# The first half of the value projection in 512-column matmuls, all of it ahead of the first attention scores

## The chip, the core and the metric

The kernel runs on one core of a Trainium2 chip. The metric is the device time of one execution in microseconds (us), the median of several runs. The engines of the core are named as in the profile: PE is TensorE (matmuls; PEld are its weight loads), DVE is VectorE, ACT is ScalarE, POOL is GpSimd, SP is SyncE, which here only issues DMAs.

## What is computed

The reference is a decoder trunk of two layers on 512 tokens of width 1024, in float32. Layer 0 mixes tokens by pooling, layer 1 by stick-breaking attention with 16 heads of 64 channels. Each layer is followed by a squared-ReLU MLP of width 4096, and every part sits between two RMS norms. What bears on the change is the shared key and value projection and the attention:

```python
kv = jnp.matmul(rms_norm(x, kv_norm_g), w_kv).reshape(B, S, 2, N_HEADS, HEAD_DIM)   # after layer 0
k = kv[:, :, 0].transpose(0, 2, 1, 3)
v = kv[:, :, 1].transpose(0, 2, 1, 3)
...
q = jnp.matmul(h, w_q[j])                                       # h = rms_norm(x, mix_pre_g)
log1m = jnp.where(mask, -jax.nn.softplus(z), 0.0)               # z = q k / 8, mask: s < t
excl = lax.cumsum(log1m, axis=3, reverse=True) - log1m
a = jnp.where(mask, jnp.exp(jax.nn.log_sigmoid(z) + excl), 0.0)
o = a @ v                                                       # per head
m = jnp.matmul(o, w_o[j])
```

## The kernel before, in words

**Numbers in two parts.** Every matmul operand is held as two tiles of a reduced float32 format, a high part (a cast on ACT) and a low part (a subtraction on DVE). A product is three matmuls: high by high, high by low, low by high. `mm3` (L299 to L302) issues them with a 128 x 128 block of activations as the loaded weights and a slice of weight columns as the moving operand; `up_block` (L703) the other way around, with weights loaded and up to 512 tokens moving.

**Weights.** The weights of the attention are read, multiplied by the norm gains, split in two parts and written back to DRAM (`kept`) during the MLP of layer 0 (`split_apart`, L207). The attention then only reads the two parts back, two DMAs of 512 KB a block (L242, on SP's queue). There are four slots for such blocks on the chip: three of the tag `w` and one of the tag `wx` (`place`, L190). `want` (L187) makes the list of blocks in the order in which the steps need them, `fill` (L246) reads the next ones while fewer than four are waiting to be used, and `get` (L253) takes one. The two blocks for the first step of the output projection are not kept; they are read raw and split on ACT and DVE (L170, L172).

**The order of attention.** The stage is a list of steps, `ATT_ORDER` (L59). The eight pairs of heads go through these steps; digits name a pair or unit, and the digits behind it token tiles of 128:

- `N2`, `N3`: the last two token tiles of the MLP's result are transposed on PE and split (`need`, L431). Tiles 0 and 1 were transposed inside the MLP's last step.
- `Vu...`: `values` (L882) for unit `u` of four heads, that is 256 columns. For a token tile it does 8 times `mm3` with 256 columns, and evacuates the PSUM bank by one cast on ACT (L897) and one subtraction on DVE (L898). A unit's weights are two blocks of four contraction chunks each.
- `K0`: `start` (L904) does the first 256 tokens of the key projection of pair 0 (24 matmuls of 256 columns), ahead of `N3`.
- `Pp`: `queries_keys` (L931) projects the keys and then the queries of pair `p`, 24 matmuls of 512 columns each (`project`, L910; for pair 0 the keys' other 256 tokens), and evacuates them with four casts and two subtractions for the keys (L936 to L938), two and two for the queries (L946, L947).
- `Sp`: `weights` (L1065): for each of the two heads, eight score matmuls (L991, L992) into three banks, sigmoids on ACT (L1000, L1012), a scan on DVE (L1016) and a multiplication on DVE (L1022).
- `Tp`: `transposed` (L1076): ten 128 x 128 transposes a head on PE (L1035) into three banks, and casts and subtractions of them (L1041, L1045).
- `Ap`: `mix_pair` (L1093): eight products with the values a head (L1052), one bank; evacuation on ACT and DVE (L1059, L1063) and a split (L281, L282).
- `Ou...`: `out_proj` (L1104): the output projection of two pairs. `E1`: the end of the stage, written out by hand.

The order on PE is written out by hand up to and including `P0` (`manual_schedule`, L1256). From there to the end step a planner of the framework sets each engine's order at build time, from the order of the program and from modelled times; the order that came of it is seen in the trace. All PSUM tiles come from one pool of 8 banks (`ps`, L123).

Of the kernel before, what the change touches and what calls it, by code (L numbers as in the profile page):

```python
# [10 lines left out]
F32 = mybir.dt.float32  # L11
F32R = mybir.dt.float32r
ACT = mybir.ActivationFunctionType
ALU = mybir.AluOpType

P = 128
D = 1024
S = 512
T = S // P
KC = D // P  # L20
# [7 lines left out]
HD = 64  # L28
# [4 lines left out]
TS = [slice(t * P, (t + 1) * P) for t in range(T)]  # L33
NS = [slice(0, 512), slice(512, 1024)]
# [23 lines left out]

ATT_ORDER = [  # L59
    (w[0], int(w[1]), [int(c) for c in w[2:]])  # L60
    for w in """V001 N2 K0 N3 V02 P0 V03 S0 P1 T0 V101 S1 A0 P2 T1 V123 A1 S2 P3 T2 O00123 A2 S3 P4 V201 T3 A3
    S4 P5 T4 V223 S5 A4 P6 V301 T5 S6 A5 V323 P7 T6 E1""".split()
]

# [37 lines left out]
C_MIX_PRE0, C_KV, C_MIX_PRE1, C_MLP_PRE1 = range(4)  # L102
# [3 lines left out]
def trunk(ctx, tc, x, consts, grow, pw, wup, wdn, wq, wk, wv, wo, out):  # L106
    nc = tc.nc
# [11 lines left out]
    def name(s):  # L119
        uid[0] += 1  # L120
        return f"{s}{uid[0]}"

    def ps():  # L123
        return psum.tile([P, 512], F32, tag="ps", name=name("ps"))
# [50 lines left out]
    def gains(lo, n):  # L175


        def scaled(raw):
            for k in range(n):
                c = raw[:, k * D // n : (k + 1) * D // n]  # L180
                nc.scalar.mul(c, c, gc[:, lo + k : lo + k + 1])  # L181

        return scaled

    gate, queue, made, ahead, dn_pool, att_pool, dn_raw = [False], [], {}, 4, [None], [None], {}

    def want(key, src, scaled=None):  # L187
        queue.append((key, src, scaled))
# [48 lines left out]
    def make():  # L237
        k, src, scaled = queue.pop(0)
        if k in kept:
            made[k] = place(k)  # L240
            for n, t in enumerate(made[k]):
                latest["sp"] = nc.sync.dma_start(t.bitcast(F32), kept[k][n])  # L242
            return
        made[k] = weight(src, place(k), scaled, dn_raw.pop(k, None))

    def fill(n=1):  # L246
        if gate[0]:
            behind.update(latest)
        for _ in range(n):
            if queue and len(made) < ahead and (queue[0][0][0] != "dn" or dn_pool[0]):  # L250
                make()

    def get(key):  # L253
        while key not in made:
            make()
        return made.pop(key)

    for l in range(2):
        if l == 1:
            n = len(queue)  # L260
            for what, i, part in ATT_ORDER:
                if what == "V" and 0 in part:
                    for h in range(2):
                        want(("v", i, h), wv[i, h], gains(C_KV * KC + 4 * h, 4))
                elif what == "P":
                    want(("k", i), wk[i], gains(C_KV * KC, KC))
                    want(("q", i), wq[i], gains(C_MIX_PRE1 * KC, KC))
                elif what == "O" or what == "E":
                    for c in range(2 * i, 2 * i + 2 if what == "O" else PAIRS):
                        want(("o", c), wo[c])  # L270
            apart.extend(x for x in queue[n:] if x[0] not in [("o", c) for c in range(2)])

            queue[n - GRP : n + GRP] = queue[n : n + GRP] + queue[n - GRP : n]
        for j in range(NJ):
            want(("up", l, j), wup[l, j])
        for j in range(NJ - GRP, NJ):
            want(("dn", l, j), wdn[l, j])
# [21 lines left out]
    def mm3(dst, ah, al, bh, bl, start, stop):  # L299
        nc.tensor.matmul(dst, ah, bh, start=start, stop=False)  # L300
        nc.tensor.matmul(dst, ah, bl, start=False, stop=False)  # L301
        nc.tensor.matmul(dst, al, bh, start=False, stop=stop)  # L302

    xnh = keep.tile([P, KC, S], F32R, tag="xnh", name="xnh")
    xnl = keep.tile([P, KC, S], F32R, tag="xnl", name="xnl")
# [125 lines left out]
    def need(*tiles):  # L431
        for t in tiles:
            if t in pending:
                pending.pop(t).transpose()
# [59 lines left out]
    def y_tiles():  # L494
        return [work.tile([P, D], F32, tag=f"y{t}", name=name(f"y{t}")) for t in range(T)]
# [207 lines left out]
    def up_block(pu, w, cols, last=False):  # L703
        wh = w[0].rearrange("p (k c) -> p k c", k=KC)
        wl = w[1].rearrange("p (k c) -> p k c", k=KC)

        def low(k):
            nc.tensor.matmul(pu[:, cols], wl[:, k, :], xnh[:, k, cols], start=False, stop=k == KC - 1)  # L708

        for k in range(KC):  # L710
            nc.tensor.matmul(pu[:, cols], wh[:, k, :], xnh[:, k, cols], start=k == 0, stop=False)  # L711
            nc.tensor.matmul(pu[:, cols], wh[:, k, :], xnl[:, k, cols], start=False, stop=False)  # L712
            if not last:
                low(k)
        if last:
            for k in range(KC):
                low(k)
# [161 lines left out]
    with tc.tile_pool(name="att", bufs=1, reuse_waits="tile") as ap:  # L879
        att_pool[0] = ap  # L880

        def values(u, part):  # L882
            if u not in vs:
                w = [get(("v", u, h)) for h in range(2)]
                vs[u] = w, ap.tile([P, T, 4, 2, HD], F32R, tag="v", bufs=2, name=name("v"))
            w, v = vs[u]
            for s in part:
                need(s)
                pv = ps()
                for k in range(KC):  # L890
                    c = slice((k % 4) * 256, (k % 4) * 256 + 256)
                    mm3(
                        pv[:, :256], xnh[:, k, TS[s]], xnl[:, k, TS[s]],
                        w[k // 4][0][:, c], w[k // 4][1][:, c], k == 0, k == KC - 1,
                    )
                pv4 = pv[:, :256].rearrange("p (h d) -> p h d", h=4)
                nc.scalar.copy(v[:, s, :, 0, :], pv4)  # L897
                nc.vector.tensor_tensor(  # L898
                    out=v[:, s, :, 1, :], in0=pv4, in1=v[:, s, :, 0, :].bitcast(F32), op=ALU.subtract
                )  # L900

        started = {}

        def start(key):  # L904

            need(0, 1)
            started[key] = ps(), get(key)
            up_block(*started[key], slice(0, S // 2))

        def project(key):  # L910
            need(*range(T))
            if key in started:
                pq, w = started.pop(key)
                up_block(pq, w, slice(S // 2, S))
            else:
                pq = ps()
                up_block(pq, get(key), slice(0, S))
            return pq

        def qk_tile(tag):  # L920
# [38 lines left out]
        with tc.issue_after(latest["pool"].ins):  # L959
            nc.gpsimd.memset(begin, 0.0)  # L960
            for lo, n in SEG.values():
                c = min(n - P, 1)
                d = begin[:, lo + n - P - c : lo + n]
                nc.gpsimd.affine_select(
                    out=d, in_=d, pattern=[[-1, P + c]], base=c - 1, channel_multiplier=1,
# [99 lines left out]
        def weights(p):  # L1065
            hs = [Head(qk[p], p, a) for a in range(2)]
            for x in hs:
                for b in range(3):
                    x.scores(b)
                    x.against(b)  # L1070
                    x.for_(b)
                x.scan()
                x.weigh()
            return hs

        def transposed(hs):  # L1076
            for x in hs:
                for b in range(3):
                    x.turn(b)
                    x.high(b)  # L1080
                    x.low(b)
# [20 lines left out]
        vs, os, wos, y = {}, {}, {}, y_tiles()  # L1102
# [119 lines left out]
        def until(key):  # L1222
            while key not in made:
                make()

        qk, heads, gpost1 = {}, {}, None

        def step(what, i, part):
            nonlocal gpost1
            if what == "V":  # L1230
                values(i, part)
            elif what == "N":
                need(i)
            elif what == "K":
                start(("k", i))
            elif what == "P":
                qk[i] = queries_keys(i)
                if i == PAIRS - 1:
                    until(("o", 5))
            elif what == "S":  # L1240
                gate[0] = True
                heads[i] = weights(i)
                fill()
            elif what == "T":
                transposed(heads[i])
                behind.update(latest)
            elif what == "A":
                mix_pair(i, vs[i // 2][1])
            elif what == "O" and part:
                out_proj(i, part)  # L1250
                if i == 0:
                    with tc.issue_after(latest["sp"].ins):
                        gpost1 = gain_row(R_MIX_POST1)

# [65 lines left out]
```

## Time and profile before

| | |
|---|---|
| Median of 3 runs | 952.17 us (951.81 to 952.43) |
| The profiled execution | 952.24 us, of which the span from first to last instruction is 950.5 us |
| Granted TensorE clock, mean over the span | 0.999 |
| First value step (V001) begins | 368.46 us into the span |
| First score of pair 0 (S0) begins | 392.91 us |
| Transposes of pair 2 (T2) begin | 454.31 us |
| First output projection (O0) begins | 456.41 us |

Times in the views are us from the start of the span. A timeline row gives the start, the time that the instruction took, the engine, the line of the kernel, the operation, what it writes and reads, the shapes and the count; in brackets stands the idle time of the engine before it and what ended it. Matmuls are pipelined, so a row's duration is longer than the distance to the next one's start; it is that distance that adds up. A windows row gives, for a stretch, the busy time of each engine and the number of its instructions.

### The profile page before, as it was taken

How to read it: one execution, taken by the hardware profiler on the slowest of the kernel's cores; microseconds unless marked ns; L12 is line 12 of the kernel's file. 1: busy time of each engine (PE TensorE's matmuls, PEld its weight loads, DVE VectorE, ACT ScalarE, POOL GpSimd, SP SyncE). 2: the span in 40 equal slices, each digit the busy share in tenths (PEclk: the TensorE clock that was granted, in tenths of full speed). 3: DMA queues.
4: the chain of work that ended last, by engine and by line, in shares of the span. 5: the costliest groups of instructions: out<-in, count | busy, mean ns of one | idle time of the engine just before them, and what ended most of it. 6: DMA issues, size and time to landing. Idle time of an engine off the chain costs nothing.

```text
span 950.5 us, 12510 instructions
## 1 busy us (share of the span) xinstructions
PE 940.9 (99%) x4758; PEld 799.7 (84%) x4758; DVE 707.9 (74%) x813; ACT 577.8 (61%) x1015; POOL 42.1 (4%) x85
## 2 busy tenths in 40 slices
PE   9999999999999999999999999999999999999996
PEld 7998888888888889899899988898888888888885
DVE  5875798988979976476577778874696966958756
ACT  6667979788775547456656554865545444444532
POOL 2300000000000004000000000200000000000002
PEclk9999999999999999999999999999999999999999
DMA  8244969789697760522424271442513233133102
GB/s 309 96 178 148 342 219 347 295 283 356 217 323 269 271 207 2 202 85 90 172 95 178 91 264 45 134 155 71 196 43 131 93 133 111 45 133 111 35 11 89
DMA packets 43262, 156.15 MB, mean 164 GB/s; under 512 B 4289, under 2 KB 4673, under 8 KB 43202
## 3 DMA queue, kind: packets, MB, share of 16 engines
q1 hardware_dynamic: 43202, 155.36, 46.1%
q8 instruction: 37, 0.61, 0.3%
q14 instruction: 23, 0.19, 0.1%
HBM read 121.79 MB, written 33.55 MB: 163 GB/s over the span
## 4 chain that ended last, share of the span: by engine, by line
PE 94%; DVE 2%; ACT 2%; POOL 1%; issue 1%; POOLq 0%; DVEq 0%; ACTq 0%
PE ps L589 28%; PE ps L708 15%; PE ps L712 15%; PE ps L711 15%; PE ps L300 4%; PE ps L301 4%; PE ps L302 4%; PE ps L1052 2%; PE ps L829 1%; PE ps L1035 1%; PE ps L991 1%; PE ps L395 1%; PE ps L992 1%; ACT xn L285 1%; PE ps L801 1%
## 5 line engine op out<-in xcount | busy, mean ns | idle before, releaser
L589 PE MATMUL ps<-w,a 128*128 128x512 f32 x1176 | 278.6, 389 | 0.0
L711 PE MATMUL ps<-xnh,w 128*128 128x512 f32 (+1 forms) x712 | 261.1, 369 | 0.0
L712 PE MATMUL ps<-xnl,w 128*128 128x512 f32 (+1 forms) x712 | 261.1, 368 | 0.0
L708 PE MATMUL ps<-xnh,w 128*128 128x512 f32 (+1 forms) x712 | 260.3, 368 | 0.1
L589 PEld LDWEIGHTS ps<-w,a 128*128 128x128 f32 x1176 | 220.7, 188 | 45.9 <-DVE w L282 0.2
L712 PEld LDWEIGHTS ps<-xnl,w 128*128 128x128 f32 x712 | 134.2, 189 | 21.8
L708 PEld LDWEIGHTS ps<-xnh,w 128*128 128x128 f32 x712 | 133.7, 189 | 22.4 <-DVE w L850 0.3
L711 PEld LDWEIGHTS ps<-xnh,w 128*128 128x128 f32 x712 | 133.8, 189 | 22.1
L598 DVE TENSOR_TENSOR y<-ps,y 128x512 f32<-128x512 f32 x124 | 84.5, 688 | 43.9 <-PE ps L589 43.7
L172 DVE TENSOR_TENSOR w<-raw,w 128x1024 fp32r<-128x1024 f32 x58 | 70.9, 1223 | 57.4 <-ACT w L170 57.2
L170 ACT CAST w<-raw 128x1024 fp32r<-128x1024 f32 x58 | 61.0, 1051 | 79.3 <-PE ps L708 79.2
L281 ACT CAST a<-r 128x768 fp32r<-128x768 f32 (+1 forms) x60 | 47.7, 794 | 72.1 <-PE ps L589 55.7
L282 DVE TENSOR_TENSOR a<-r,a 128x768 fp32r<-128x768 f32 (+1 forms) x60 | 54.1, 902 | 12.3 <-ACT a L281 12.1
L281 ACT CAST w<-e 128x1536 fp32r<-128x1536 f32 (+1 forms) x30 | 41.8, 1394 | 23.8 <-DVE e L563 14.4
L1016 DVE TENSOR_TENSOR_SCAN e<-u,begin 128x1280 f32<-128x1280 f32 x16 | 45.2, 2823 | 11.0 <-ACT u L1000 10.4
L282 DVE TENSOR_TENSOR w<-e,w 128x1536 fp32r<-128x1536 f32 (+1 forms) x30 | 49.5, 1649 | 1.8 <-ACT w L281 1.6
L181 ACT ACTIVATE apart<-apart,eye 128x128 f32<-128x128 f32 (+1 forms) x132 | 43.1, 407 | 0.5 <-DMA apart<-in_wk 0.5
L282 DVE TENSOR_TENSOR w<-w,w 128x1536 fp32r<-128x1536 f32 (+1 forms) x20 | 33.0, 1650 | 8.6 <-ACT w L281 8.6
L621 ACT ACTIVATE r<-ps 128x512 f32<-128x512 f32 x56 | 33.1, 591 | 8.6 <-PE ps L708 8.5
L282 DVE TENSOR_TENSOR w<-xn,w 128x1536 fp32r<-128x1536 f32 (+1 forms) x20 | 33.0, 1650 | 5.6 <-ACT w L281 5.5
L300 PE MATMUL ps<-w,xnh 128*128 128x256 f32 x128 | 36.6, 286 | 0.0
L622 ACT ACTIVATE r<-r 128x512 f32<-128x512 f32 x56 | 35.5, 634 | 1.3
(134 smaller groups left out, 1393.6 us busy)
## 6 DMA issues: line engine op xcount, KB each, us to landing
raw<-in_wup SPq DMA_DIRECT2D x64, 512.0 KB, 4.1
w<-kept SPq DMA_DIRECT2D x60, 512.0 KB, 4.2
kept<-wx SPq DMA_DIRECT2D x30, 512.0 KB, 5.0
w<-in_wdn SPq DMA_DIRECT2D x8, 1536.0 KB, 6.7
kept<-apart SPq DMA_DIRECT2D x24, 512.0 KB, 5.7
xn<-in_wdn SPq DMA_DIRECT2D x8, 1536.0 KB, 7.7
apart<-in_wk SPq DMA_DIRECT2D x7, 512.0 KB, 7.1
apart<-in_wq SPq DMA_DIRECT2D x7, 512.0 KB, 9.4
```

What stands on the lines that cost most here:

```text
L170: nc.scalar.copy(hi, raw)
L172: nc.vector.tensor_tensor(out=lo, in0=raw, in1=hi.bitcast(F32), op=ALU.subtract)
L181: nc.scalar.mul(c, c, gc[:, lo + k : lo + k + 1])
L281: latest["act"] = nc.scalar.copy(hi, src)
L282: latest["dve"] = nc.vector.tensor_tensor(out=lo, in0=src, in1=hi.bitcast(F32), op=ALU.subtract)
L300: nc.tensor.matmul(dst, ah, bh, start=start, stop=False)
L589: nc.tensor.matmul(bank, a[:, x, q, TS[t]], w[:, z, q], start=start and q == 0 and k == 0, stop=q == self.n - 1 and k == 2, skip_group_che ...
L598: nc.vector.tensor_tensor(out=part, in0=bank, in1=part, op=ALU.add)
L708: nc.tensor.matmul(pu[:, cols], wl[:, k, :], xnh[:, k, cols], start=False, stop=k == KC - 1)
L711: nc.tensor.matmul(pu[:, cols], wh[:, k, :], xnh[:, k, cols], start=k == 0, stop=False)
L712: nc.tensor.matmul(pu[:, cols], wh[:, k, :], xnl[:, k, cols], start=False, stop=False)
L1016: nc.vector.tensor_tensor_scan(out=self.e[:, ::-1], data0=self.u[:, 1:][:, ::-1], data1=begin[:, ::-1], initial=0.0, op0=ALU.mult, op1=ALU ...
```

## The change

`V0` and `V1`, the values of the first eight heads, become two steps `H0` and `H1`, and go ahead of everything else. `half_values` projects 512 columns at once, with `mm3` on whole banks. Its four weight blocks hold two contraction chunks of 512 columns each, where before a block had four chunks of 256. All four are taken at the first step and fill the four slots. `H0` does chunks 0 to 3 of a token tile, `H1` chunks 4 to 7 into the same bank, which is then evacuated in two pieces of 256 columns by the same casts and subtractions as before. `K0` is gone: `P0` projects the keys in one go. `V2` and `V3` stay as they were. The gains of the new blocks are two multiplications of 512 columns each in place of four of 256. At the last `H` step `fill(ahead)` asks for up to four blocks.

```diff
-    for w in """V001 N2 K0 N3 V02 P0 V03 S0 P1 T0 V101 S1 A0 P2 T1 V123 A1 S2 P3 T2 O00123 A2 S3 P4 V201 T3 A3
+    for w in """H001 N2 H101 N3 H023 H123 P0 S0 P1 T0 S1 A0 P2 T1 S2 A1 P3 T2 O00123 A2 S3 P4 V201 T3 A3
     S4 P5 T4 V223 S5 A4 P6 V301 T5 S6 A5 V323 P7 T6 E1""".split()
...
-                if what == "V" and 0 in part:
+                if what == "H" and not i and 0 in part:
+                    for h in range(4):
+                        want(("v", 0, h), wv[h], gains(C_KV * KC + 2 * h, 2))
+                elif what == "V" and 0 in part:
                     for h in range(2):
-                        want(("v", i, h), wv[i, h], gains(C_KV * KC + 4 * h, 4))
+                        want(("v", i, h), wv[2 * i + h], gains(C_KV * KC + 4 * h, 4))
...
+        def value_parts(v, s, src):
+            pv4 = src.rearrange("p (h d) -> p h d", h=4)
+            nc.scalar.copy(v[:, s, :, 0, :], pv4)
+            nc.vector.tensor_tensor(
+                out=v[:, s, :, 1, :], in0=pv4, in1=v[:, s, :, 0, :].bitcast(F32), op=ALU.subtract
+            )
+
+        half_w, half_bank = [], {}
+
+        def half_values(i, part):
+            if not half_w:
+                half_w.extend(get(("v", 0, h)) for h in range(4))
+                for u in range(2):
+                    vs[u] = None, value_tile(u)
+            for s in part:
+                if i == 0:
+                    half_bank[s] = ps()
+                for k in range(4 * i, 4 * i + 4):
+                    (wh, wl), c = half_w[k // 2], NS[k % 2]
+                    mm3(
+                        half_bank[s], xnh[:, k, TS[s]], xnl[:, k, TS[s]], wh[:, c], wl[:, c], k == 0, k == KC - 1
+                    )
+                if i == 1:
+                    for u in range(2):
+                        value_parts(vs[u][1], s, half_bank[s][:, u * 256 : u * 256 + 256])
+            if i == 1 and T - 1 in part:
+                fill(ahead)
...
         def project(key):
-            need(*range(T))
-            if key in started:
-                pq, w = started.pop(key)
-                up_block(pq, w, slice(S // 2, S))
-            else:
-                pq = ps()
-                up_block(pq, get(key), slice(0, S))
+            pq = ps()
+            up_block(pq, get(key), slice(0, S))
             return pq
```

`start` and its `K` step are removed, `values` calls `value_parts`, and the host lays the value weights out to match. Nothing ahead of the attention's first step and nothing from `O0` on changes in the list of steps.

More of the change, by code (lines that the diff above doesn't have):

```diff
@@ L267, in trunk @@
                     want(("q", i), wq[i], gains(C_MIX_PRE1 * KC, KC))
-                elif what == "O" or what == "E":
+                elif what == "O" and 0 in part or what == "E":
                     for c in range(2 * i, 2 * i + 2 if what == "O" else PAIRS):
@@ L880, in trunk, with value_tile @@
         att_pool[0] = ap
+        def value_tile(u):
+            return ap.tile([P, T, 4, 2, HD], F32R, tag="v", bufs=2, name=name("v"))
+        def value_parts(v, s, src):
[23 more added lines that the diff above has]
+                fill(ahead)
         def values(u, part):
             if u not in vs:
-                w = [get(("v", u, h)) for h in range(2)]
-                vs[u] = w, ap.tile([P, T, 4, 2, HD], F32R, tag="v", bufs=2, name=name("v"))
+                vs[u] = [get(("v", u, h)) for h in range(2)], value_tile(u)
             w, v = vs[u]
             for s in part:
-                need(s)
                 pv = ps()
@@ L895, in values @@
                     )
[L896 to L908, printed above, removed]
-        def project(key):
-            need(*range(T))
-            if key in started:
-                pq, w = started.pop(key)
-                up_block(pq, w, slice(S // 2, S))
-            else:
-                pq = ps()
-                up_block(pq, get(key), slice(0, S))
+                value_parts(v, s, pv[:, :256])
+        def project(key):
+            pq = ps()
+            up_block(pq, get(key), slice(0, S))
             return pq
@@ L1229, in step @@
             nonlocal gpost1
-            if what == "V":
+            if what == "H":
+                half_values(i, part)
+            elif what == "V":
                 values(i, part)
@@ L1233, in step @@
                 need(i)
-            elif what == "K":
-                start(("k", i))
             elif what == "P":
@@ L1250, in step @@
                 out_proj(i, part)
-                if i == 0:
+                if gpost1 is None:
                     with tc.issue_after(latest["sp"].ins):
@@ L1289 @@
     blocks = lambda w, n: w.reshape(KC, P, -1, n).transpose(2, 1, 0, 3)
-    wv = blocks(a["w_kv"][:, D:], 256).reshape(4, P, 2, D).transpose(0, 2, 1, 3)
+    wv = np.concatenate([
+        blocks(w, n).reshape(-1, P, c, D).transpose(0, 2, 1, 3).reshape(4, P, D)
+        for w, n, c in ((a["w_kv"][:, D : D + 512], 512, 4), (a["w_kv"][:, D + 512 :], 256, 2))
+    ])
     arrays = {
```

## The prediction

> **What bounds the kernel now.** The page comes first.
>
> ```profile
> PE 940.9 (99%) x4758; PEld 799.7 (84%) x4758; DVE 707.9 (74%) x813; ACT 577.8 (61%) x1015; POOL 42.1 (4%) x85
> ...
> PE 94%; DVE 2%; ACT 2%; POOL 1%; issue 1%; POOLq 0%; DVEq 0%; ACTq 0%
> ```
>
> PE has work nearly all the time, and the chain that ended last runs over PE for 94%. So two things can move the time: fewer PE microseconds, or new waits of PE. The windows by stage, with columns PE, PEld, DVE, ACT, tell where waits would come from:
>
> ```profile
> 368.46:392.91 24.45, 24.45 (x186) 23.49 (x184) 10.93 (x18) 11.62 (x25) 6.45 (x23) 1.00 0.19 69
> 392.91:406.37 13.46, 13.46 (x66) 11.35 (x65) 9.65 (x6) 7.60 (x19) 0.00 (x0) 1.00 0.74 269
> 406.37:430.35 23.98, 23.98 (x149) 21.65 (x148) 17.55 (x20) 14.22 (x32) 0.00 (x0) 1.00 0.25 88
> 430.35:454.31 23.96, 23.96 (x150) 21.66 (x149) 17.51 (x20) 14.59 (x33) 0.00 (x0) 1.00 0.24 89
> ```
>
> The first is the lead-in up to the first score; the others end where T0, T1 and T2 begin. PE never pauses, and in the last two DVE is busy 17.5 of 24 us. Those two each hold half of V1, which the change takes out.
>
> **What PE saves.** The distance between starts is the price of a matmul in a stream:
>
> ```profile
> 473.09 0.40 PE L711 MATMUL ps<-xnh,w 128*128 128x512 f32 x1
> ...
> 483.99 0.28 PE L300 MATMUL ps<-w,xnh 128*128 128x256 f32 x1
> ...
> 489.74 2.35 PE L1035 MATMUL ps<-eye,w 128*128 128x128 f32 x20
> ```
>
> Between the first two rows stand P3's 48 matmuls of 512 columns: 10.90 / 48 = 0.2271 us. Between the last two stand 48 value matmuls of 256 columns (half of V2): 5.75 / 48 = 0.1198 us. V0 and V1 are 2 units x 4 tiles x 8 chunks x 3 = 192 of the small ones, 23.00 us. They become 96 of the large ones, 21.80 us: 1.20 us less. P0's keys, before 24 + 24 small ones (5.75 us), become 24 large ones (5.45 us): 0.30 us less. Together PE saves **1.5 us**, 0.16% of the time. The Trainium skill, in "TensorE: Matmul & The Clock Gate", section "Back-to-back issue gap", gives a warm gap of N / 2.4 ns plus 2.5 ns; by that, 120 pairs of small ones joined would save only an estimated 0.3 us, and the sum below would be 953.0. The trace's distances are wider than the page's at both sizes, and they decide.
>
> Of the rest of the value work nothing goes: per tile and unit there is still a cast of 128 x 256 on ACT and a subtraction on DVE, 16 each in all. The gain multiplications are halved in number, in the MLP of layer 0 where ACT is not what PE waits for; nothing.
>
> **The lead-in.** H001 takes 24 large matmuls, 5.45 us from 368.46, to 373.9. H101 takes as long after N2, and so N3 comes later than before.
>
> ```profile
> 374.21 1.04 PE L395 MATMUL ps<-eye,xn 128*128 128x128 f32 x8
> ...
> 377.95 1.04 PE L395 MATMUL ps<-eye,xn 128*128 128x128 f32 x8
> ...
> 375.81 1.34 ACT L385 ACTIVATE xn<-x,stat 128x512 f32<-128x512 f32 x2
> ...
> 379.20 1.29 DVE L414 TENSOR_TENSOR xnl<-ps,xnh 128x512 fp32r<-128x512 f32 x2 [2.45 <-ACT xnh L405]
> ```
>
> N2 and N3 stood at 374.21 and 377.95, with no wait. Tile 3's norm ended at 377.15, and N3 now comes at 373.9 + 0.8 + 5.45 = 380.1: covered. Its low part ended 2.5 us after N3's start; H023 does tile 2 first, for 2.72 us after the 0.8 of the transposes, so even with the two casts and subtractions of tile 1's values ahead of it there is cover. H023 ends at 386.4, H123 at 391.8, P0 at 402.7.
>
> P0's weights are new on the path. Before, k0 and q0 had slots of their own; now the values hold all four. k0's DMAs wait on SP until its slot is free, which H023's second chunk of tile 3 does at 383.7 + 1.4 = 385.1, 6.7 us ahead of P0. The same wait in the trace of before (k1, behind the first part of P0):
>
> ```profile
> 384.57 0.40 PE L711 MATMUL ps<-xnh,w 128*128 128x512 f32 x1
> ...
> 384.76 0.80 SPq L242 DMA_DIRECT2D w<-kept  x2
> ...
> DMA to landing us min/median/max: 3.2/3.7/4.1
> ```
>
> The issue came 0.2 us behind the last reader, and the second part landed 0.4 + 4.1 us after that: 4.7 us in all, so 2 us are to spare. Queued behind k0 on SP are q0, k1 and q1, needed 5 us later or more. Cost nothing; the cover is H123.
>
> **The first scores lose their cover.** V03 stood between P0 and S0:
>
> ```profile
> 390.04 0.28 PE L300 MATMUL ps<-w,xnh 128*128 128x256 f32 x1
> ...
> 390.85 0.68 DVE L947 TENSOR_TENSOR q<-ps,q 64x512 fp32r<-64x512 f32 x1 [2.25 <-ACT q L946]
> 392.18 0.69 DVE L947 TENSOR_TENSOR q<-ps,q 64x512 fp32r<-64x512 f32 x1 [0.65 <-ACT q L946]
> ...
> 392.91 0.39 PE L991 MATMUL ps<-k,q 128*128 128x512 f32 x1
> ...
> 394.19 0.40 PE L991 MATMUL ps<-k,q 128*128 128x512 f32 x1
> ```
>
> P0 ended at 390.04. The queries of head 0 were whole at 391.53, those of head 1 at 392.87, and V03 covered just that (head 1's scores begin 1.28 us behind head 0's). Without it PE waits 1.5 us, unless the planner puts matmuls of P1 there, whose weights have landed. That it moves work of a later step ahead is seen in T3, A3, S4:
>
> ```profile
> 492.38 0.57 PE L1052 MATMUL ps<-ah,v 128*128 128x384 f32 x2
> 492.79 0.39 PE L991 MATMUL ps<-k,q 128*128 128x512 f32 x1
> 493.25 0.33 PE L1052 MATMUL ps<-al,v 128*128 128x384 f32 x1
> ```
>
> S4's first scores (L991) stand ahead of products of A3 (L1052), which the program has first. I take it that P1 fills the gap; the 1.5 us are then not lost but S0 starts that much later.
>
> **DVE in pairs 0 to 2.** V101 and V123 also stood behind T0 and T1, where they covered this:
>
> ```profile
> 404.83 0.68 DVE L938 TENSOR_TENSOR kl<-ps,k 64x512 fp32r<-64x512 f32 x1
> 406.76 0.69 DVE L938 TENSOR_TENSOR kl<-ps,k 64x512 fp32r<-64x512 f32 x1 [1.25 <-ACT k L937]
> 407.48 0.68 DVE L947 TENSOR_TENSOR q<-ps,q 64x512 fp32r<-64x512 f32 x1
> 408.20 1.62 DVE L1045 TENSOR_TENSOR al<-ps,ah 128x512 fp32r<-128x512 f32 x3
> 409.85 0.69 DVE L947 TENSOR_TENSOR q<-ps,q 64x512 fp32r<-64x512 f32 x1
> ...
> 408.47 0.36 PE L300 MATMUL ps<-w,xnh 128*128 128x256 f32 x1
> ```
>
> T0 took PE from 406.37 to 408.47, where V101 began. Head 1's queries were whole at 410.54, 0.8 us past the place where S1 now wants them (408.47 + 1.28 for head 0). Again P2 or A0 can fill. What can't be filled for ever is DVE's queue. From the first score to T2 DVE has 9.65 + 17.55 + 17.51 = 44.7 us of work, of which five value subtractions (2.1 us, group below) go: 42.6. PE's time there falls from 61.4 by two halves of V1 (11.6) to 49.8, and DVE's first scan comes 3.06 us after the first score (395.97 - 392.91): 46.7 us for 42.6.
>
> ```profile
> L898 DVE TENSOR_TENSOR v<-ps,v 128x256 fp32r<-128x256 f32 x5 | 2.1, 423 | 5.5 <-ACT v L897 5.5
> L938 DVE TENSOR_TENSOR kl<-ps,k 64x512 fp32r<-64x512 f32 x5 | 3.4, 679 | 2.5 <-ACT k L937 2.5
> L947 DVE TENSOR_TENSOR q<-ps,q 64x512 fp32r<-64x512 f32 x4 | 2.8, 688 | 0.7 <-ACT q L946 0.6
> L1063 DVE TENSOR_TENSOR o<-ps,o 64x512 f32<-64x512 f32 x4 | 2.7, 677 | 1.7 <-ACT o L1059 1.6
> ...
> 395.97 2.83 DVE L1016 TENSOR_TENSOR_SCAN e<-u,begin 128x1280 f32<-128x1280 f32 x1 [2.03 <-ACT u L1000]
> ...
> 452.53 0.66 DVE L938 TENSOR_TENSOR kl<-ps,k 64x512 fp32r<-64x512 f32 x1
> ...
> 455.38 1.23 DVE L172 TENSOR_TENSOR w<-raw,w 128x1024 fp32r<-128x1024 f32 x1
> ```
>
> Of the 4.1 us to spare, 1.5 go to the later S0 and 1.2 to the second split of O0's weights (455.38, behind T2's start before), which can now come earlier: 1.4 are left. Against them stand DVE's waits for ACT in this stretch, 2.5 + 0.7 + 1.7 = 4.9 us. If none is filled with other work PE loses 3.5 us by T2; if all are, nothing. The row at 452.53, a key subtraction set between a scan and its multiplication, is of the second kind, so I take the nearer end: **1.1 us lost**. Where DVE is that late PE is held at T2 and behind it, as it was a little already:
>
> ```profile
> 457.66 0.40 PE L302 MATMUL ps<-w,ohl 128*128 128x512 f32 x1
> 458.10 0.50 PE L300 MATMUL ps<-w,ohl 128*128 128x512 f32 x1
> ```
>
> O0's second bank came 0.2 us late there (0.44 in place of 0.23). After O0, 10.9 us of PE alone, DVE has caught up and all goes on as before.
>
> **The sum**, against the profiled execution of 952.24 us, which is 0.07 above the median: -1.5 + 1.1 = -0.4, **951.8 us**. What a measurement of this kernel can tell from no change is about 0.2%, 1.9 us, and PE's saving is less than that.
>
> **Rivals.**
>
> *All cover holds.* DVE keeps up and PE loses nothing: 952.24 - 1.5 = 950.7, and with O0's wait and the small ones around it gone 950.3. For it speaks that PE has no wait in the 61 us of the last three windows; against it that V101 and V123 were 11.6 us in which DVE had 5.5 us of idle time (first group row).
>
> *The gaps stay open (slower).* The planner's order keeps S behind P with nothing between. The price is 1.5 us at S0, 0.8 at S1 and as much at S2, 3.1, and the DVE shortage of up to 3.5 on top; in the middle 4.9, with the saving +3.4: **955.6**. It decides from 1.5 us of lost PE time on; it is measurably slower from 3.4. For it speaks that a plan made with modelled times can be off by the few tenths that a gap of 1.5 us is made of (O0's row); against it the mixed order at 492.
>
> *P0's weights come late (slower).* If k0's DMAs go only when all of H123 is done, or behind a blocked DMA on SP, PE waits the 4.7 us of the k1 rows at 391.8, with P1 unable to fill since its weights are behind. That is -1.5 + 1.1 + 4.7: 956.5. Against it speaks the k1 row, issued 0.2 us after its own slot's last reader. The skill's page named above, section "HAM oscillation — how this bites in real kernels", warns of PE gaps beyond about 3.4 us, after which the clock falls to half; the windows above show no gap at all and a clock of 1.00, so no row here tests it.
>
> **How the numbers follow.** Forecast 0.52 (its own range 950.7 to 954.2, from a loss of 0 to 3.5), cover holds 0.12, gaps open 0.26, weights late 0.10. Faster by over 0.2% means under 950.3: half of "cover holds", 0.06. Slower by over 0.2% means above 954.1: weights late 0.10, most of the open gaps 0.21, the edge of the forecast 0.02, together 0.33. Within: 0.61. The range from 950.4 to 956.6 leaves out half of "cover holds", half of "weights late" and the worst of the open gaps.
>
> **What would show it.** Right: in the new trace 96 matmuls of L300's kind with 512 columns at 0.227, the stretch from the first H to the end of P0 34.2 us long with no wait, some matmuls of P1 ahead of S0, of P2 ahead of S1, and DVE busy over 90% from the first scan to T2. Wrong: a PE wait at the first matmul of P0 (weights), at L991 of S0 to S2 (queries), or at T1 and T2 for DVE's multiplication L1022. If PE's wait there sums to over 3.4 us, my reading of DVE's slack or of the planner is what failed.

## The result: 0.8% slower

The changed kernel takes **959.33 us** (median of 4 runs, 958.41 to 960.46) against 952.2 us (951.81 to 952.43) before. The ratio is 1.0078, with a 95% interval of 1.0065 to 1.009. The prediction was 951.8 us, range 950.4 to 956.6: the measured time lies 2.7 us above it. The four runs lie in two groups, 958.4 and 958.5 at a mean granted clock of 0.999, 960.2 and 960.5 at 0.997; the profiled one is of the second group (960.16 us, span 958.4 us).

**The page after.** First the busy times, then the shares of the chain that ended last, then one group (line, instruction, count | busy us, mean ns | idle time before it and what ended it).

```profile
PE 943.1 (98%) x4638; PEld 794.8 (83%) x4638; DVE 708.4 (74%) x813; ACT 575.7 (60%) x1007; POOL 42.2 (4%) x85
...
PE 90%; DVE 4%; ACT 3%; POOL 1%; issue 1%; POOLq 0%; DVEq 0%; ACTq 0%
...
L592 PE MATMUL ps<-w,a 128*128 128x512 f32 x1176 | 279.7, 390 | 2.4 <-ACT a L284 2.4
```

PE has 120 matmuls fewer, as the diff says, but its share of the chain fell from 94% to 90%: PE waits now. The third line shows the first wait, and it isn't in attention at all. L592 is the down projection of an MLP, and it waits 2.4 us for a cast on ACT.

**Where the 7.9 us went**, from the two profiled executions, by the points at which the same work begins:

| Stretch | before | after | difference |
|---|---|---|---|
| start of the span to the first value step | 368.46 | 372.58 | +4.12 |
| first value step to T2 | 85.85 | 89.98 | +4.13 |
| T2 to the end of the execution | 497.93 | 497.60 | -0.33 |
| sum | 952.24 | 960.16 | +7.92 |

*The first row* is the MLP of layer 0, where the step list is the same. These are the rows of PE there (the view of the timeline), after:

```profile
181.13 0.39 PE L715 MATMUL ps<-xnl,w 128*128 128x512 f32 x1
181.35 0.39 PE L711 MATMUL ps<-xnh,w 128*128 128x512 f32 x1
184.09 1.88 PE L592 MATMUL ps<-w,a 128*128 128x512 f32 x4 [2.35 <-ACT a L284]
185.77 0.63 PE L714 MATMUL ps<-xnh,w 128*128 128x512 f32 x1
186.19 0.63 PE L715 MATMUL ps<-xnl,w 128*128 128x512 f32 x1
...
187.84 0.39 PE L711 MATMUL ps<-xnh,w 128*128 128x512 f32 x1
188.07 0.40 PE L714 MATMUL ps<-xnh,w 128*128 128x512 f32 x1
```

From 181.35 the next start should come 0.23 us later; it comes 2.74 later, so 2.51 us are lost. Then the matmuls start 0.42 to 0.43 us apart instead of 0.227: from 184.09 to 187.84 are 9 of them, 3.75 us where 2.04 are due, 1.7 us more. Together that is 4.2, the row's 4.12 to 0.1. The rows of ACT say why, before and after:

```profile
179.18 0.84 ACT L281 CAST a<-r 128x768 fp32r<-128x768 f32 x1 [1.97 <-DVE r L544]
181.54 1.06 ACT L170 CAST w<-raw 128x1024 fp32r<-128x1024 f32 x1 [1.52 <-PE ps L708]
```

```profile
181.78 1.04 ACT L170 CAST w<-raw 128x1024 fp32r<-128x1024 f32 x1 [4.32 <-PE ps L711]
182.73 0.59 ACT L624 ACTIVATE r<-ps 128x512 f32<-128x512 f32 x1
183.22 0.82 ACT L284 CAST a<-r 128x768 fp32r<-128x768 f32 x1
```

Before, the activations' cast `a` came ahead of a weight cast, `w`, that has to wait until PE frees its slot. After, `w` is ahead in ACT's queue, ACT sits idle for 4.32 us behind it, and `a` comes 4.0 us later. Of these, DVE makes the first 2.2: the subtraction that gives `a` its input (`r`) has another place in DVE's queue too. Before and after:

```profile
178.19 0.95 DVE L544 TENSOR_TENSOR r<-r 128x768 f32<-128x768 f32 x1
```

```profile
180.43 0.95 DVE L547 TENSOR_TENSOR r<-r 128x768 f32<-128x768 f32 x1
```

So `a` could have begun at 181.4 and been whole at 182.2, when PE would have waited about 0.7 us for it instead of 2.5 (an estimate from these rows, since PE wants it at 181.58). The weight cast ahead of it, and the activation behind that, made the start 183.22.

*The second row*: the waits of PE, less the saving. From 400 to 450 us the view of waits has these two lines (us in total, times, longest), where before it had none:

```profile
PE ps L1008 <- DVE q L964: 2.7, 4, 1.4
PE ps L1008 <- DVE al L1062: 0.9, 1, 0.9
```

L1008 is the first score matmul of a row of tiles. `q` is its operand; `al` is the low part of the transposed weights, and the subtraction that makes it reads a PSUM bank, which a score needs next. By the distances between starts, which hold the short waits too, PE loses 1.7 us at S0, 1.0 at S1 and 3.0 at S2 with the place just ahead of it, 5.7 in all. The end of P0 and the start of S0, with nothing put between:

```profile
406.78 0.39 PE L711 MATMUL ps<-xnh,w 128*128 128x512 f32 x1
408.56 0.50 PE L1008 MATMUL ps<-k,q 128*128 128x512 f32 x1 [1.39 <-DVE q L964]
408.89 0.39 PE L1009 MATMUL ps<-kl,q 128*128 128x512 f32 x1
```

The windows (PE, PEld, DVE, ACT, POOL busy, clock, DMA share, GB/s) of the lead-in, then from the first score to T0, T0 to T1, T1 to T2:

```profile
372.58:406.78 34.20, 34.20 (x161) 28.50 (x159) 11.66 (x21) 12.22 (x28) 6.45 (x23) 1.00 0.43 154
...
408.56:422.19 13.63, 13.63 (x65) 11.52 (x65) 10.01 (x6) 7.74 (x19) 0.00 (x0) 1.00 0.40 149
422.19:441.36 19.17, 18.77 (x101) 15.85 (x100) 16.52 (x18) 13.57 (x31) 0.00 (x0) 1.00 0.16 56
441.36:462.56 21.20, 19.47 (x101) 15.82 (x100) 19.26 (x20) 14.86 (x31) 0.00 (x0) 1.00 0.14 51
```

The lead-in is 34.2 us without a wait, as forecast. In the last window DVE is busy for 19.26 of 21.20 us, 91%, where before it was 17.51 of 23.96, 73%. The worst place is S2, first on DVE and then on PE:

```profile
442.19 1.23 DVE L172 TENSOR_TENSOR w<-raw,w 128x1024 fp32r<-128x1024 f32 x1 [0.25 <-ACT w L170]
443.44 0.68 DVE L964 TENSOR_TENSOR q<-ps,q 64x512 fp32r<-64x512 f32 x1
444.16 1.62 DVE L1062 TENSOR_TENSOR al<-ps,ah 128x512 fp32r<-128x512 f32 x3
445.81 0.69 DVE L964 TENSOR_TENSOR q<-ps,q 64x512 fp32r<-64x512 f32 x1
446.53 1.22 DVE L172 TENSOR_TENSOR w<-raw,w 128x1024 fp32r<-128x1024 f32 x1
447.79 1.62 DVE L1062 TENSOR_TENSOR al<-ps,ah 128x512 fp32r<-128x512 f32 x3
```

```profile
444.18 0.50 PE L1008 MATMUL ps<-k,q 128*128 128x512 f32 x1 [0.47 <-DVE q L964]
...
446.65 0.47 PE L1008 MATMUL ps<-k,q 128*128 128x512 f32 x1 [0.41 <-DVE q L964]
...
448.53 0.39 PE L1008 MATMUL ps<-k,q 128*128 128x256 f32 x1 [0.85 <-DVE al L1062]
```

The two splits of the output projection's weights (L172) stand ahead of `q` and of `al`, and PE stops three times. Before, one of them lay between two scans (448.66) and the other behind T2's start.

*The third row* is O0: the 0.2 us by which its second bank came late before, and the slower start behind it, are gone.

### The profile page after: what moved, and what is told of

Its sections match the earlier page's. It is cut to its first block, busy times and chain, and to the rows that moved or that the text cites. A ratio compares the mean times of both kernels' runs of the same rounds, so it can differ in the third digit from the quotient of the medians.

```text
span 958.4 us, 12263 instructions
## 1 busy us (share of the span) xinstructions
PE 943.1 (98%) x4638; PEld 794.8 (83%) x4638; DVE 708.4 (74%) x813; ACT 575.7 (60%) x1007; POOL 42.2 (4%) x85
## 4 chain that ended last, share of the span: by engine, by line
PE 90%; DVE 4%; ACT 3%; POOL 1%; issue 1%; POOLq 0%; DVEq 0%; ACTq 0%
PE ps L592 28%; PE ps L711 14%; PE ps L714 14%; PE ps L715 14%; PE ps L303 4%; PE ps L305 4%; PE ps L304 4%; PE ps L1069 2%; PE ps L832 1%; PE ps L1052 1%; PE ps L398 1%; DVE e L1033 1%; ACT xn L288 1%; PE ps L804 1%; PE ps L1008 1%
## 5 line engine op out<-in xcount | busy, mean ns | idle before, releaser
L592 PE MATMUL ps<-w,a 128*128 128x512 f32 x1176 | 279.7, 390 | 2.4 <-ACT a L284 2.4
L592 PEld LDWEIGHTS ps<-w,a 128*128 128x128 f32 x1176 | 221.0, 188 | 48.6 <-ACT a L284 2.8
L172 DVE TENSOR_TENSOR w<-raw,w 128x1024 fp32r<-128x1024 f32 x58 | 70.8, 1222 | 58.7 <-ACT w L170 58.7
L181 ACT ACTIVATE apart<-apart,eye 128x128 f32<-128x128 f32 (+2 forms) x122 | 41.3, 418 | 0.2 <-DMA apart<-in_wk 0.2
L288 ACT ACTIVATE xn<-y 128x512 f32<-128x512 f32 (+1 forms) x25 | 15.3, 613 | 32.2 <-DVE y L470 28.6
```

The source lines that it names most:

```text
L172: nc.vector.tensor_tensor(out=lo, in0=raw, in1=hi.bitcast(F32), op=ALU.subtract)
L592: nc.tensor.matmul(bank, a[:, x, q, TS[t]], w[:, z, q], start=start and q == 0 and k == 0, stop=q == self.n - 1 and k == 2, skip_group_che ...
```

## The experiments

The theory after the result: three causes that add up, the saving of PE (-1.5), a wait from the new order of the weight preparation (+4.1 in the profiled execution), and scores that lost their cover (+5.7, and -0.3 at O0). Rivals were that PE saves almost nothing; that one cause feeds the other; and that DVE, not the missing cover, is what holds the pairs. Run beside the experiments, the kernel before always lay between 951.25 and 952.62 us, its medians between 951.99 and 952.06.

**e1: the preparation as before.** Its list of blocks is put back in the order of before, with four gain multiplications a block.

```diff
-                        want(("v", 0, h), wv[h], gains(C_KV * KC + 2 * h, 2))
+                        want(("v", 0, h), wv[h], gains(C_KV * KC + 2 * h, 2, 4))
...
             apart.extend(x for x in queue[n:] if x[0] not in [("o", c) for c in range(2)])
+            apart[2:8] = apart[4:8] + apart[2:4]
```

The new last argument of `gains` is the number of multiplications.

> The changed kernel, with the weights prepared in the MLP of layer 0 in the order of before (v, v, k, q, k, q, v, v) and with four gain multiplications of 256 columns a value block; the attention is that of the changed kernel. Theory: of the 7.9 us between the two profiled executions, about 4 were lost in the MLP of layer 0 (a wait of 2.5 us at 181.35 for a cast on ACT, and slow matmuls behind it), because the other kinds of blocks in the preparation made the planner set that cast behind another one. Here that goes, and only the attention's part stays: 952.2 - 1.5 + 5.4 of waits at S0, S1, S2 = about 956.0, and no PE wait near 181 us. Rival: the wait in the MLP has nothing to do with the order of preparation (chance of a run, or a matter of code size): 959 as the changed kernel.

Measured 955.63 us (955.47 to 956.48), ratio 1.0040 [1.0027, 1.0052]. The wait at 181 us is gone, those at S0 to S2 are as after. The products that waited follow the row at 181.13 by 0.23 us now:

```profile
181.13 0.39 PE L713 MATMUL ps<-xnh,w 128*128 128x512 f32 x1
181.36 1.07 PE L594 MATMUL ps<-w,a 128*128 128x512 f32 x4
```

The preparation is worth 3.7 us between the medians, the rest of the change 3.6.

**e2: the kernel before, with the preparation as after.** The first four value blocks come first, with only two of their four gain columns each; the other two are left out.

```diff
-                        want(("v", i, h), wv[i, h], gains(C_KV * KC + 4 * h, 4))
+                        want(("v", i, h), wv[i, h], gains(C_KV * KC + 4 * h, 4 if i > 1 else 2))
...
             apart.extend(x for x in queue[n:] if x[0] not in [("o", c) for c in range(2)])
+            apart[2:8] = apart[6:8] + apart[2:6]
```

> The mirror: the kernel before, with the weights prepared in the order of the changed kernel (four value blocks first) and two gain multiplications of 512 columns for the first four value blocks, so that these blocks get only two of their four gain columns; the attention is that of before. Theory: the 2.5 us wait at 181 us appears with the attention unchanged, and where the clock falls behind it 1.5 us more: 954.7 to 956.4. Rival: the attention's change causes it: 952.2.

Measured 954.87 us (954.16 to 956.72), ratio 1.0032 [1.0020, 1.0045]. The profiled execution, 956.72 us, has the wait at the same place:

```profile
184.10 1.88 PE L590 MATMUL ps<-w,a 128*128 128x512 f32 x4 [2.35 <-ACT a L282]
```

Attention is that of before, so this cause stands alone. Between the medians it is worth 2.8 us here, against 3.7 in e1. The profiled execution is the longest of the five and has the slow matmuls behind the wait; whether the shorter ones have them isn't shown.

**e12, e13: the order of the blocks or the shape of the multiplications?** e1 undid both. e12 has only e1's change of `apart`, e13 only its four multiplications.

> The changed kernel with the blocks prepared in the order of before (two value blocks, then k and q of pairs 0 and 1, then the other two value blocks), the gain multiplications left at two of 512 columns. Theory (the order of the blocks makes the wait): no wait of PE at 181 us, the time of e1, 955.6 us (955.2 to 956.6). Rival (the shape of the multiplications does): about 959 us as the changed kernel, or a wait of PE for ScalarE at another place of the MLP of layer 0.

> The changed kernel with four gain multiplications of 256 columns per value block in place of two of 512, the order of the blocks left as changed. Theory (the order of the blocks makes the wait): PE waits 2.5 us for ScalarE's cast at 181 us as in the changed kernel, 958.4 to 960.5 us. Rival (the shape does): 955.6 us.

e12 took 955.82 us (955.41 to 956.18), e13 960.24 us (958.94 to 960.50). The row of e13:

```profile
184.21 2.08 PE L593 MATMUL ps<-w,a 128*128 128x512 f32 x4 [2.35 <-ACT a L285]
```

It is the order of the blocks alone. The number of gain multiplications costs nothing that these runs show, as predicted, but the order in which blocks are prepared was never looked at. How the planner gets from that list to the other order on ACT and DVE isn't shown.

**e3: what PE saves.** e1 with each value matmul of 512 columns as two of 256, whose halves of a bank take turns. (The values don't come out right in this form; it serves for the time alone.)

> As e1, but each 512-column value matmul is done as two of 256 columns, in the same place: the move alone, without the merging. Theory, from 0.1198 and 0.2271 us a matmul: 1.2 us over e1, 957.2. Rival, from the page's gap rule named in the prediction: 0.3 us over e1, 956.3.

Measured 957.22 us (956.48 to 957.38), 1.6 us over e1, and the two profiled executions differ by as much. In these, 0.4 us of it arose ahead of the first value matmul (368.11 in e1, 368.49 in e3). From N3's transposes to P0's first matmul, with half of the value matmuls between, e1 and then e3:

```profile
379.89 1.03 PE L400 MATMUL ps<-eye,xn 128*128 128x128 f32 x8
...
391.66 0.39 PE L716 MATMUL ps<-xnh,w 128*128 128x512 f32 x1
```

```profile
380.86 1.04 PE L400 MATMUL ps<-eye,xn 128*128 128x128 f32 x8
...
393.24 0.40 PE L716 MATMUL ps<-xnh,w 128*128 128x512 f32 x1
```

12.38 less 11.77 is 0.61 us for half of them, 1.2 for all: the size that the prediction took from the trace, not the 0.3 that it worked out from the Trainium skill.

**e4: half of the next pair's keys as cover.** e1 with a step `Kp` that does four of eight key chunks of the next pair ahead of the scores; the order stays with the planner.

```diff
-    ... P0 S0 P1 T0 S1 A0 P2 T1 S2 A1 P3 T2 O00123
+    ... P0 K1 S0 P1 T0 K2 S1 A0 P2 T1 K3 S2 A1 P3 T2 O00123
```

> As e1, with half of the next pair's key matmuls (contraction chunks 0 to 3, 12 matmuls of 512 columns, 2.7 us) put by the step list between P0 and S0, T0 and S1, T1 and S2, and the other half left at P1, P2, P3: no matmul more or fewer. Theory (lost cover): the waits for the queries go, 1.55 at S0, 0.7 at S1, about 1.2 at S2, and the rest at S2 comes from DVE's weight splits and stays: 3.5 under e1, 952.5, with at most 0.5 us of new wait at T0. Rival (DVE's queue is the bound in pairs 0 to 2): the waits come back at T1, T2 or O0, and the time is within 1 us of e1.

Measured 961.02 us (959.93 to 961.56): both theories missed. The planner put all 24 key matmuls of P1 ahead of S0, which began at 408.75. No wait there, but at T0:

```profile
417.44 1.31 PE L1064 MATMUL ps<-eye,w 128*128 128x128 f32 x10 [0.53 <-DVE w L1051]
423.42 2.37 PE L1064 MATMUL ps<-eye,w 128*128 128x128 f32 x10 [4.67 <-DVE w L1051]
```

The matmuls behind the second wait then ran at half rate for a while (last section), and PE stood still once more, 1.78 us at 446.35, for a cause that the trace doesn't show. Cover is needed on both sides of the scores: ahead of them for the queries, behind them for the scan and the multiplication of both heads on DVE. What is moved to one side is missing on the other.

**e5 to e8: short cover, written by hand.** e5 is e1 with PE's order by hand up to P3 (a control). e6 puts 2, 3 and 4 key chunks ahead of S0, S1 and S2. e7 is e1 with the two output weight blocks held back until S2 is issued. e8 is e6 and e7 together.

```diff
-        first = [what for what, _, _ in ATT_ORDER].index("P") + 1
+        first = ATT_ORDER.index(("P", 3, [])) + 1
...
+    ... P0 K12 S0 P1 T0 K23 S1 A0 P2 T1 K34 S2 A1 P3 T2 O00123
...
-            if queue and len(made) < ahead and
+            if queue and (queue[0][0] not in [("o", 0), ("o", 1)] or 2 in heads) and len(made) < ahead and
```

> e1 with PE's order written by hand up to the projections of pair 3, in place of only up to pair 0; no work is added or moved but the first two matmuls of P3, which the planner had put ahead of A1's last. A control for the two runs beside it that need a hand order. Both theories expect the time of e1: 955.6 us (955.0 to 956.3), with the same waits of PE: about 1.6 us ahead of S0, 1.2 at S1 and 3.0 at S2.

> e5 with the first chunks of the next pair's key projection as cover ahead of the scores, moved there from P1, P2 and P3: 2 chunks (6 matmuls, 1.4 us) ahead of S0, 3 (2.0 us) ahead of S1, 4 (2.7 us) ahead of S2; the work of PE is the same. Theory (PE only lacks independent work between a projection and its scores, and each chunk count is about the wait that it covers, so that the scores start no later than in e5): the waits at S0, S1 and S2 fall from 5.8 us together to under 1, T0 to T2 wait for nothing new, time 950.0 to 951.5. Rival (VectorE's chain sets the pace of a pair, and the waits only move): S0 to S2 without wait, but T0 to T2 wait as in e4, 954 us or more.

> e1 with the loading and splitting of the first two output weight blocks held back until the scores of pair 2 are issued, so that their two splits on VectorE (1.2 us each) no longer lie ahead of q and al at S2. Theory (of the 3.0 us that PE waits at S2, the part that these splits delay is 1.6 to 2, the rest is the missing cover): S2's wait falls to 1.0 to 1.4, T2 may wait up to 1.2 for the first split which now lies ahead of its scan, time 953.6 to 955.0. Rival (the missing cover alone makes the wait): 955.6 as in e1.

> e6 and e7 together. Theory: if e6 leaves no wait at S2, holding the splits back gives nothing more and may cost up to 1 us at T2 (950.0 to 952.0); if e6 leaves 1 us or more there, this takes it away. Rival (VectorE sets the pace): slower than e7.

| | us (range) | ratio [95%] | PE lost at S0, S1, S2 and just ahead | at T2 and O0 |
|---|---|---|---|---|
| e1 | 955.63 (955.47 to 956.48) | 1.0040 [1.0027, 1.0052] | 1.7, 1.0, 3.0 | 0.4 |
| e5 | 955.83 (955.73 to 956.15) | 1.0041 [1.0027, 1.0054] | 1.7, 1.1, 3.0 | 0.4 |
| e6 | 952.88 (952.61 to 953.11) | 1.0009 [1.0000, 1.0018] | 0.4, 0.7, 1.5 | 0.4 |
| e7 | 954.37 (953.99 to 955.49) | 1.0027 [1.0017, 1.0036] | 1.7, 1.1, 0.8 | 1.5 |
| e8 | 953.32 (952.73 to 954.60) | 1.0015 [1.0006, 1.0024] | 0.4, 0.7, 0.1 | 2.2 |

e5 is e1: the hand order by itself does nothing. In e6 most of the time comes back, 2.9 of the 3.8 us that e5 lies over before, by moving 27 matmuls that PE does anyway: the missing cover was the cause of that part. But 1.4 to 2.9 us more were expected. A part of what is left is a wait for the bank of the first chunk, behind the transposes:

```profile
419.24 0.47 PE L716 MATMUL ps<-xnh,w 128*128 128x512 f32 x1 [0.21 <-PE ps L1060]
```

e7 took 2.2 us from S2, so the weight splits made most of that wait, but 1.1 came back at O0. e8 shows the same: with S2 clean, T2 and O0 lose 1.8 us more.

**e9 to e11: room on DVE?** e9 is e6 with only the second output block held. e10 is e9 with K2 and K3 (3 chunks each) ahead of T0 and T1. e11 is e10 with 2 chunks each.

```diff
+    ... P0 K12 S0 P1 K23 T0 S1 A0 P2 K33 T1 S2 A1 P3 T2 O00123
```

> e6 with the second output weight block alone held back until the scores of pair 2 are issued; the first is split where e6 splits it. Theory (in e6 the 0.8 us at S2 and part of the 0.6 us ahead of them come from the second split on VectorE at 441.4 us; in e8 it was the second block's place ahead of T2's last evictions that cost 1.7 us, and the place just ahead of S2's first scan cost nothing): S2 without wait, T2 and O0 as in e6, 951.6 to 952.3. Rival (VectorE has no room anywhere in pairs 1 and 2): the wait moves to T2, 952.8 or more.

> e9 with the key chunks of pairs 2 and 3 (3 each) put ahead of the transposes T0 and T1 instead of behind them, so that VectorE's q subtractions come ahead of the transposes' evictions, and the chunks' bank is not waited for behind them (0.4 and 0.6 us in e6). Theory: S0 to S2 wait under 0.8 us together, T0 to T2 nothing, 950.8 to 951.8. Rival (the evictions of T0 and T1 then come later than S1 and S2 need them or their banks): waits of 1 us or more at S1 and S2, 952.5 or more.

> e10 with 2 chunks at each place instead of 2, 3 and 3. Theory: 0.7 us less cover at S1 and S2, where e10 has at most as much to spare: 0 to 1.4 us over e10. Rival (cover ahead of the transposes is spare, it only makes T0 and T1 later): the time of e10 or less.

e9 took 952.85 us (952.65 to 953.32), ratio 1.0009 [1.0000, 1.0018]. S2 is without wait, as the theory had it, but the time is the rival's and no better than e6: a wait came up, not at T2, but at the start of O0.

```profile
457.26 0.47 PE L305 MATMUL ps<-w,ohl 128*128 128x512 f32 x1 [0.55 <-DVE kl L963]
```

The windows from T1 to T2 of e6 and of e9:

```profile
435.62:455.36 19.74, 19.00 (x102) 15.82 (x101) 18.27 (x20) 14.07 (x30) 0.00 (x0) 1.00 0.15 54
```

```profile
435.50:454.36 18.86, 18.45 (x101) 15.92 (x100) 17.43 (x19) 13.96 (x30) 0.00 (x0) 1.00 0.15 57
```

DVE works for 18.27 of 19.74 and 17.43 of 18.86 us, 93% and 92%; before it was 73%. When a pair has nothing but its own work and these splits, DVE has little room in it, and a wait that is taken away at one place can come up at the next. e10 took 954.65 us (954.44 to 955.09) and e11 954.91 us (954.83 to 956.06), ratios 1.0028 [1.0017, 1.0038] and 1.0033 [1.0020, 1.0046]. The rival of e10 holds: S2 waits for the queries again, behind the transposes this time.

```profile
441.69 0.50 PE L1016 MATMUL ps<-k,q 128*128 128x512 f32 x1 [0.78 <-DVE q L972]
```

e11, with less cover, waits 2.2 us for the queries of S1 and S2 in place of 0.9, as its theory has it, yet by the medians it is only 0.3 us slower, since a wait of 0.7 us at the start of O0 is gone.

No version beats the kernel before: the best, e6 and e9, keep PE's saving and win back more than half of what the scores lost, and are still 0.8 us over it.

## Why the prediction was wrong

- **PE's saving: right.** 1.2 us for the values by e3. The waits of 5.7 less the table's 4.13 leave about 1.5 for values and keys together. (The 48 large matmuls that gave the price are P4's by the step list, not P3's; the price is the same.)
- **"In the MLP of layer 0 where ACT is not what PE waits for; nothing": the first step that failed.** It counted the instructions and not the order in which they come. Four value blocks now stand at the head of the preparation; the planner's order of ACT came out differently, one cast, itself 2.2 us later by DVE's order, got behind another that has to wait for PE, and PE lost 2.5 us and, in the profiled execution, 1.7 more in slow matmuls. e12 and e13 show that the order of the blocks does this alone. No rival named it, and without it the time (955.6, e1) is inside the range.
- **The lead-in and P0's weights: right.** 34.2 us without a wait. The rival *P0's weights late* is out.
- **"I take it that P1 fills the gap": the second step that failed.** S0's first matmul lost 1.5 us, the price worked out for an open gap, and nothing was put there. The rows of S4 among A3 showed that the planner can mix steps, not that it does where a wait comes. Why it left S0's gap open while it put two matmuls of P3 ahead of A1's last three isn't settled.
- **DVE in pairs 0 to 2: mis-sized, and in kind.** I took 4.1 us of spare time over the whole stretch and set waits against that, 1.1 lost. But T0, T1 and T2 don't wait, and S1 and S2 lose 4.0 us: what comes late is `q` and `al` a few tenths to one us behind T, whatever spare time DVE has later. The second weight split was counted as work, "can now come earlier", 1.2 us of DVE's time; its place ahead of `al` cost PE 1.0 us directly, and e7 gives 2.2 for both at S2. The rival *The gaps stay open* had the mechanism: 3.1 us plus 0 to 3.5, middle 4.9, against 5.7 measured. That e1's 955.63 falls on its 955.6 is luck in part: S2 lost 3.0 us where it had 0.8, the larger part through the weight splits, and the shortage up to T2 that it put at 0 to 3.5 doesn't appear at T0 to T2.
- **The clock.** After the 2.35 us wait the matmuls ran at half rate (next section), which had been left out since no row before had a gap.

## What to carry to other kernels

Work that looks like a detour between two dependent steps may be their cover: before it is moved, list what each engine has to finish between the producer's last and the consumer's first instruction, and compare that with what stays in between, place by place, not as a sum over the stage. Where a planner sets the order, a change of any list that it works from (here the order of weight blocks, used 190 us later) can reorder queues elsewhere; check the order of each engine in every stage that handles the moved items. An engine at 73% in a stage may be at over 90% when the other engine's work is taken out of it.

## What the runs showed of the hardware

A wait of PE of 2.35 us was followed by matmuls at about half the rate. The window around it, after:

```profile
180.00:190.00 10.00, 7.65 (x27) 5.85 (x26) 10.00 (x11) 8.19 (x15) 0.00 (x0) 0.83 0.57 176
```

The granted clock is 0.83 over these 10 us, and the starts lie 0.42 to 0.43 us apart for some 3.5 us. e2 and e13 show it behind the same wait. The Trainium skill, "TensorE: Matmul & The Clock Gate", section "Wait — 56ns, not 53.3ns?", has 426.7 ns for 512 columns on the cold array: the rows agree.

e4's wait of 4.67 us was followed by such a stretch too (the window around it, then three of its matmuls):

```profile
417.00:429.00 12.00, 6.89 (x33) 6.02 (x34) 9.92 (x12) 3.98 (x9) 0.00 (x0) 0.86 0.25 89
...
426.01 0.63 PE L717 MATMUL ps<-xnl,w 128*128 128x512 f32 x1
426.44 0.57 PE L713 MATMUL ps<-xnh,w 128*128 128x512 f32 x1
426.84 0.39 PE L716 MATMUL ps<-xnh,w 128*128 128x512 f32 x1
```

The shorter waits were not: behind 1.39 us at S0 and behind 1.78 us in e4 the starts are 0.23 us apart again after the first. The Trainium skill, "TensorE: Matmul & The Clock Gate", section "HAM oscillation — how this bites in real kernels", sets the bound at gaps of more than about 3.4 us; here 2.35 us sufficed in all three traces that have this wait. Whether it does each time isn't shown: the runs of the changed kernel at a clock of 0.999 are 1.7 to 2 us shorter than those at 0.997, as if they lacked the slow matmuls, but only one run of it was traced, and e2 has a run of 954.16 us at 0.997, which doesn't fit.
